# Four instead of three weight pairs by seven products in a SwiGLU unit, their sums written over the loaded words, gate and up completed in PSUM

## The chip, the cores and the metric

The kernel runs on one core of one Trainium2 chip. The metric is the device time of one execution in microseconds. The core has five engines with instruction queues of their own: TensorE (PE, with its weight loads as PEld), VectorE (DVE), ScalarE (ACT), GpSimd (POOL) and SyncE (SP), which here only issues transfers. Each engine executes its queue in the order in which the program was built, and waits at an instruction until the semaphores that it names have come.

## The reference

A hybrid encoder with two layers on 256 tokens of width 2048. Each layer has a mixer (neighbourhood attention with a gated recurrence in layer 0; pooling with grouped attention in layer 1) and then a SwiGLU of hidden width 5632. The change is in the SwiGLU alone:

```
def swiglu(x, w_gate, w_up, w_down):
    return (jax.nn.silu(x @ w_gate) * (x @ w_up)) @ w_down

    x = layer_norm(DN_ALPHA * x + y, ln_mix_g[layer], ln_mix_b[layer])
    f = swiglu(x, ffn_w_gate[layer], ffn_w_up[layer], ffn_w_down[layer])
    x = layer_norm(DN_ALPHA * x + f, ln_ffn_g[layer], ln_ffn_b[layer])
```

## The kernel before

**Numbers in two halves.** Every fp32 operand is split into a high part (a cast to fp32r, on ACT) and a low part (the difference, on DVE), by `split` (L126). A product of two such operands is three matmuls (`mm3`, L287): low by high, high by high, high by low. A matmul is 128 x 128 by 128 x 512. So each weight word that is loaded costs a cast on ACT and a subtraction on DVE before TensorE can use it.

**Chunks and phases.** The hidden width is cut into eleven chunks of 512 columns. `ffn` (L501) takes them in three phases per layer (`PHASES`, L69): three chunks, four, four. After the chunks of a phase come its down projections, which add to the residual. In the first phase a chunk is done by `whole` (L505), gate and up one after the other. In the second and third phase a chunk is a `unit` (L453), which makes gate and up together for both token tiles. There are two layers with two such phases of four units: four stretches, sixteen units.

**A unit.** It has four accumulators, one PSUM bank each: c11 and c21 (gate of the two token tiles), c12 and c22 (up). The contraction over 2048 is cut into eight pairs of 128 rows. A pair is done in one of two ways.

- *By halves*: two loads of 512 KB (`load_half`, L152; tiles raw, whi, wlo), each split by one cast and one subtraction of 128x1024, and eight products, which are 24 matmuls.
- *By seven products* (a scheme of Winograd's kind for a 2 x 2 block product, token tiles and column blocks of x by rows of gate and up): one load of 1 MB (`load_seven`, L431; tile rs), seven weight words instead of four (tiles sh and sl), seven products, which are 21 matmuls. Products p1, p5, p6, p7 go to four side banks; the other three go straight to c11, c12 and c21. The left sides e, f, g, h are made from x once per layer by `forms_of` (L407; tile fm).

`SEVEN` (L72) names the pairs that are done by seven products: 5, 6 and 7. `PAIRS_FIRST`, `PAIRS` and `PAIRS_LAST` (L73 to L75) give the order of the pairs in the first unit of a phase, in the two inner ones, and in the last. L546 sets the pairs by seven products: `SEVEN[:-1]` in the last unit, `SEVEN` in all others.

**load_seven before** (L437 to L447). The words arrive in rs, which has one buffer. ACT casts three words of 512 columns (L442, 128x1536). DVE makes four sums in a tile of its own, z (L443 to L445: 128x1024, 128x512, 128x512), and then the low parts of the first three words (L446). Then the sums are split: a cast of 128x2048 and a subtraction of 128x2048. sh and sl have two buffers each.

**End of a unit** (L481 to L499). ACT copies p1 out of PSUM (L483). DVE then makes ten instructions of 128x512: sums of p1, p5, p6, p7 with the four accumulators into the tiles g0, g1, u0, u1, and two multiplications of silu(gate) by up (L497). ACT takes silu twice (L489, L492). The result of each token tile is transposed by TensorE (`transpose4`, L272, L124) into a side bank and split into yTh and yTl. This is put off by `later`: the first token tile's transposes are called after two halves of the next unit, the second one's after three (L499); a half is counted by `half_done` (L480), and seven products don't count.

**Banks.** The eight banks are two sides of four. The accumulators of a unit are one side, and p1, p5, p6, p7 the other, which is also the side of the two transposed results of the unit before. After a unit the sides change places (L495). The four side banks are asked for at the first pair by seven products (L470).

**What sets the order.** A scheduler orders the instructions of each engine when the program is built, with the priorities of `tc.high_priority` and by a timeline of its own. A buffer is taken again as soon as its last reader is done.

Of the kernel before, what the change touches and what calls it, by code (L numbers as in the profile page):

```python
# [11 lines left out]
F32 = mybir.dt.float32  # L12
# [6 lines left out]
P = 128  # L19
T = 256  # L20
NT = T // P
D = 2048
KT = D // P
NCH = 512
# [56 lines left out]
def trunk(ctx: ExitStack, tc: tile.TileContext, a, out):  # L81
# [44 lines left out]
    def split(hi, lo, src):  # L126
        nc.scalar.copy(hi, src)  # L127
        return nc.vector.tensor_tensor(lo, src, hi.bitcast(F32), op=sub).ins  # L128
# [302 lines left out]
    def load_seven(sp, src, behind):  # L431

        with ExitStack() as order:
            order.enter_context(tc.high_priority(offset=400))
            if behind:
                order.enter_context(tc.issue_after(behind))
            raw = sp.tile([P, 4, NCH], F32, tag="rs", name="rs", bufs=1)  # L437
            hi = sp.tile([P, 7, NCH], F32R, tag="sh", name="sh", bufs=2)
            lo = sp.tile([P, 7, NCH], F32R, tag="sl", name="sl", bufs=2)
            z = sp.tile([P, 4, NCH], F32, tag="z", name="z", bufs=1)  # L440
            last_load[0] = nc.sync.dma_start(raw, src).ins
            nc.scalar.copy(hi[:, :3], raw[:, :3])  # L442
            nc.vector.tensor_tensor(z[:, :2], raw[:, 0:3:2], raw[:, 3:4].to_broadcast([P, 2, NCH]), op=add)  # L443
            nc.vector.tensor_tensor(z[:, 2], z[:, 0], raw[:, 2], op=add)
            nc.vector.tensor_tensor(z[:, 3], z[:, 2], raw[:, 1], op=add)  # L445
            nc.vector.tensor_tensor(lo[:, :3], raw[:, :3], hi[:, :3].bitcast(F32), op=sub)  # L446
            split(hi[:, 3:], lo[:, 3:], z)  # L447
        return lambda i: (hi[:, i, :], lo[:, i, :])


    SEVEN_ORDER = ((0, "11", "p1"), (5, "f", "p6"), (3, "e", "p5"), (4, "g", "p7"), (1, "12", "c11"), (2, "h", "c12"), (6, "22", "c21"))

    def unit(sp, pairs, sevens, w, lhs, forms, yT, opening):  # L453

# [12 lines left out]
        for p in pairs:  # L467
            if p in sevens:
                if "p1" not in b:
                    b.update((n, side_bank(True)) for n in ("p1", "p6", "p5", "p7"))  # L470
                wt = load_seven(sp, w[p], behind.pop(0))
                for i, x, name in SEVEN_ORDER:
                    product(name, forms[p][x], wt(i))
            else:
# [4 lines left out]
                            product(f"c{tok + 1}{n + 1}", lhs(tok, ks[kk]), (hi[:, kk, :], lo[:, kk, :]))  # L479
                    half_done()  # L480
        with tc.high_priority(offset=1000):  # L481
            g0, w_, v, x = (sp.tile([P, NCH], F32, tag=n, name=n, bufs=1) for n in ("g0", "g1", "u0", "u1"))
            nc.scalar.copy(g0, b["p1"])  # L483
            nc.vector.tensor_tensor(w_, g0, b["p6"], op=sub)
            nc.vector.tensor_tensor(v, w_, b["p5"], op=add)
            nc.vector.tensor_tensor(w_, w_, b["p7"], op=add)
            nc.vector.tensor_tensor(x, w_, b["p5"], op=add)
            nc.vector.tensor_tensor(g0, g0, b["c11"], op=add)
            nc.scalar.activation(g0, g0, AF.Silu)  # L489
            nc.vector.tensor_tensor(v, b["c12"], v, op=sub)  # L490
            nc.vector.tensor_tensor(w_, w_, b["c21"], op=add)
            nc.scalar.activation(w_, w_, AF.Silu)  # L492
            nc.vector.tensor_tensor(x, b["c22"], x, op=sub)

            banks["side"] ^= 1  # L495
            for tok, (g, u) in enumerate(((g0, v), (w_, x))):
                nc.vector.tensor_tensor(g, g, u, op=mult)  # L497
                s = slice(tok * P, (tok + 1) * P)
                later.append([2 + tok, lambda g=g, s=s: transpose4(g, yT[0][:, :, s], yT[1][:, :, s], 1000)])  # L499
# [651 lines left out]
```

## Time and profile before

| | us |
|---|---|
| median of 3 runs (2194.17 to 2198.57) | 2197.3 |
| the profiled execution | 2194.88 |
| its span, first to last instruction | 2193.1 |
| loads of raw from in_gu, 512 KB each | 264 loads, 4.7 from issue to landing |
| loads of rs from in_gu, 1 MB each | 44 loads, 5.7 from issue to landing |

The profile is one execution with every instruction's start and duration, the engine, the line of the code and the tiles that it writes and reads. A group's mean is the duration of one instruction; neighbouring instructions of an engine can overlap, so that their starts lie closer together than their durations. A duration can't be added up where this is so: the distance of starts is then the price of one more. The 44 loads of rs are the pairs by seven products: eleven in each of the four stretches. In the span TensorE reads sh from 736 to 871 us, 994 to 1131 us, 1688 to 1823 us and 1946 to 2081 us: these are the four stretches, each some 20 us after its first matmul.

### The profile page before, as it was taken

The numbers are of one execution on the slowest core, as the hardware profiler recorded it, in microseconds if no ns is written. First come the engines' busy times: TensorE is split into PE (matmuls) and PEld (weight loads), VectorE is DVE, ScalarE is ACT, GpSimd is POOL, SyncE is SP. The second block draws the span as 40 slices with busy tenths as digits, with TensorE's granted clock in tenths as the row PEclk, the third lists the DMA queues.
The fourth block names the chain that finished last, engine by engine and source line by source line (L and its number), as shares of the span: only waits on it lengthen the run. The fifth ranks groups of instructions, "written<-read, shape, count | busy, mean of one in ns | idle before, by whom it ended". The sixth has DMA issues, their size and how long they took to land.

```text
span 2193.1 us, 26619 instructions
## 1 busy us (share of the span) xinstructions
PE 2172.0 (99%) x10048; PEld 1804.2 (82%) x10048; DVE 1558.9 (71%) x1952; ACT 1050.4 (48%) x1276; POOL 55.4 (3%) x51
## 2 busy tenths in 40 slices
PE   8999999999999999999999999999999999999997
PEld 7888888888888888888888888888888888888886
DVE  6885688577537787577776776667367896768865
ACT  6445534545435455444445554455335454445441
POOL 0000001000000000000000200000000000000000
PEclk9999999999999999999999999999999999999999
DMA  8555546684736565565548553646456555655573
GB/s 290 162 163 182 167 132 192 197 284 141 234 121 220 187 205 191 189 232 184 194 151 299 171 189 115 223 161 244 150 175 234 181 189 191 220 183 191 176 258 106
DMA packets 112562, 420.64 MB, mean 192 GB/s; under 512 B 13744, under 2 KB 16304, under 8 KB 105520
## 3 DMA queue, kind: packets, MB, share of 16 engines
q1 hardware_dynamic: 112432, 418.93, 57.2%
q8 instruction: 79, 1.29, 0.2%
q14 instruction: 51, 0.42, 0.1%
HBM read 416.78 MB, written 2.10 MB: 191 GB/s over the span
## 4 chain that ended last, share of the span: by engine, by line
PE 93%; DVE 3%; DMA 2%; ACT 1%; issue 1%; SPq 0%; ACTq 0%; DVEq 0%
PE acc L290 45%; PE bside L290 22%; PE aside L290 20%; PE mx L720 1%; DMA raw<-in_gu 1%; DVE wlo L128 1%; PE tr L124 1%; PE mx L290 1%; DMA rs<-in_gu 1%; ACT whi L127 1%; PE mx L766 0%; PE aside L124 0%; PE bside L124 0%; PE mx L976 0%; DVE sl L128 0%
## 5 line engine op out<-in xcount | busy, mean ns | idle before, releaser
L128 DVE TENSOR_TENSOR wlo<-raw,whi 128x1024 fp32r<-128x1024 f32 (+1 forms) x673 | 817.7, 1224 | 439.2 <-ACT whi L127 432.6
L127 ACT CAST whi<-raw 128x1024 fp32r<-128x1024 f32 (+1 forms) x673 | 703.7, 1051 | 818.6 <-PE acc L290 321.9
L290 PE MATMUL acc<-whi,xTl 128*128 128x512 f32 x1056 | 416.7, 395 | 6.7 <-DVE xTl L128 5.5
L290 PE MATMUL acc<-whi,xTh 128*128 128x512 f32 x1056 | 414.6, 393 | 0.0
L290 PE MATMUL acc<-wlo,xTh 128*128 128x512 f32 x1056 | 412.6, 393 | 0.3 <-DVE wlo L128 0.3
L290 PEld LDWEIGHTS acc<-whi,xTl 128*128 128x128 f32 x1056 | 198.9, 188 | 46.9 <-ACT whi L127 6.9
L290 PEld LDWEIGHTS acc<-wlo,xTh 128*128 128x128 f32 x1056 | 199.0, 188 | 41.1 <-DVE wlo L128 0.7
L290 PEld LDWEIGHTS acc<-whi,xTh 128*128 128x128 f32 x1056 | 199.1, 189 | 38.7
L290 PE MATMUL acc<-whi,yTl 128*128 128x512 f32 x512 | 200.7, 392 | 0.1
L290 PE MATMUL acc<-whi,yTh 128*128 128x512 f32 x512 | 199.7, 390 | 0.0
L290 PE MATMUL acc<-wlo,yTh 128*128 128x512 f32 x512 | 197.8, 390 | 0.0
L290 PE MATMUL bside<-whi,xTl 128*128 128x512 f32 x336 | 131.4, 391 | 0.9 <-ACT g L483 0.7
L290 PE MATMUL aside<-whi,xTl 128*128 128x512 f32 x336 | 131.3, 391 | 0.1
L290 PE MATMUL bside<-whi,xTh 128*128 128x512 f32 x336 | 131.0, 390 | 0.0
L290 PE MATMUL aside<-whi,xTh 128*128 128x512 f32 x336 | 131.0, 390 | 0.0
L290 PE MATMUL aside<-wlo,xTh 128*128 128x512 f32 x336 | 128.1, 390 | 0.0
L290 PE MATMUL bside<-wlo,xTh 128*128 128x512 f32 x336 | 128.1, 390 | 0.0
L290 PEld LDWEIGHTS acc<-wlo,yTh 128*128 128x128 f32 x512 | 96.1, 188 | 20.5 <-DVE wlo L128 0.5
L290 PEld LDWEIGHTS acc<-whi,yTl 128*128 128x128 f32 x512 | 96.1, 188 | 19.8 <-DVE yTl L982 0.3
L290 PEld LDWEIGHTS acc<-whi,yTh 128*128 128x128 f32 x512 | 96.2, 188 | 19.3
L128 DVE TENSOR_TENSOR sl<-z,sh 128x2048 fp32r<-128x2048 f32 x44 | 100.7, 2288 | 6.2 <-ACT sh L127 5.6
L442 ACT CAST sh<-rs 128x1536 fp32r<-128x1536 f32 x44 | 65.2, 1483 | 73.3 <-DMA rs<-in_gu 34.6
(260 smaller groups left out, 3117.4 us busy)
## 6 DMA issues: line engine op xcount, KB each, us to landing
raw<-in_gu SPq DMA_DIRECT2D x264, 512.0 KB, 4.7
raw<-in_down SPq DMA_DIRECT2D x176, 512.0 KB, 3.7
raw<-in_ab_in SPq DMA_DIRECT2D x127, 512.0 KB, 4.1
rs<-in_gu SPq DMA_DIRECT2D x44, 1024.0 KB, 5.7
raw<-in_cd_in SPq DMA_DIRECT2D x40, 512.0 KB, 4.3
raw<-in_ab_out SPq DMA_DIRECT2D x32, 512.0 KB, 4.4
raw<-in_cd_out SPq DMA_DIRECT2D x32, 512.0 KB, 4.4
x<-in_xT SPq DMA_DIRECT2D x8, 256.0 KB, 5.9
```

The source lines that it names most:

```text
L124: return nc.tensor.transpose(o, src, eye)
L127: nc.scalar.copy(hi, src)
L128: return nc.vector.tensor_tensor(lo, src, hi.bitcast(F32), op=sub).ins
L290: ins = nc.tensor.matmul(o, lhs[a], rhs[b], start=start and n == 0, stop=stop and n == 2)
L442: nc.scalar.copy(hi[:, :3], raw[:, :3])
L720: nc.tensor.matmul(m[:, 2 * h + s, :], kk[:, h, s * P : (s + 1) * P], qq[:, h, r * P : (r + 1) * P], start=True, stop=True,)
```

## The change

Three things are changed.

1. `SEVEN` becomes (4, 5, 6, 7), and the inner units take their pairs in the order 0, 4, 1, 5, 2, 6, 3, 7. Two new names, `SEVEN_FIRST` and `SEVEN_LAST`, are not used anywhere. The line that chooses the pairs of a unit is as it was, so that the first and the inner units have four pairs by seven products and the last has three: 15 in each stretch, 60 in all, in place of 44. The forms e, f, g, h are made for four pairs.
2. In `load_seven` the tile z is gone. The first three words are split first, and then the four sums are written over the loaded words in rs, which now has two buffers (xs and fs of `forms_of` use them too).
3. At the end of a unit u0 and u1 are gone: c11, c12, c21 and c22 get the sums in PSUM, silu reads PSUM, and the last multiplications read up from PSUM. The side banks are asked for in the order p1, p6, p7, p5.

```
-SEVEN = (5, 6, 7)
+SEVEN = (4, 5, 6, 7)
+SEVEN_FIRST = (5, 6, 7)
+SEVEN_LAST = (5, 6)
 PAIRS_FIRST = (0, 1, 2, 3, 5, 4, 6, 7)
-PAIRS = (0, 1, 5, 2, 3, 6, 4, 7)
+PAIRS = (0, 4, 1, 5, 2, 6, 3, 7)
 PAIRS_LAST = (0, 1, 5, 2, 6, 3, 4, 7)
...
-        xs = sp.tile([P, NT, 2 * n, P], F32, tag="rs", name="xs", bufs=1)
-        fs = sp.tile([P, 4, n, P], F32, tag="z", name="fs", bufs=1)
+        xs = sp.tile([P, NT, 2 * n, P], F32, tag="rs", name="xs", bufs=2)
+        fs = sp.tile([P, 4, n, P], F32, tag="rs", name="fs", bufs=2)
...
-            raw = sp.tile([P, 4, NCH], F32, tag="rs", name="rs", bufs=1)
+            raw = sp.tile([P, 4, NCH], F32, tag="rs", name="rs", bufs=2)
...
-            z = sp.tile([P, 4, NCH], F32, tag="z", name="z", bufs=1)
             last_load[0] = nc.sync.dma_start(raw, src).ins
-            nc.scalar.copy(hi[:, :3], raw[:, :3])
-            nc.vector.tensor_tensor(z[:, :2], raw[:, 0:3:2], raw[:, 3:4].to_broadcast([P, 2, NCH]), op=add)
-            nc.vector.tensor_tensor(z[:, 2], z[:, 0], raw[:, 2], op=add)
-            nc.vector.tensor_tensor(z[:, 3], z[:, 2], raw[:, 1], op=add)
-            nc.vector.tensor_tensor(lo[:, :3], raw[:, :3], hi[:, :3].bitcast(F32), op=sub)
-            split(hi[:, 3:], lo[:, 3:], z)
+            split(hi[:, :3], lo[:, :3], raw[:, :3])
+
+            nc.vector.tensor_tensor(raw[:, 0:4:3], raw[:, 0:3:2], raw[:, 3:4].to_broadcast([P, 2, NCH]), op=add)
+            nc.vector.tensor_tensor(raw[:, 2], raw[:, 0], raw[:, 2], op=add)
+            nc.vector.tensor_tensor(raw[:, 1], raw[:, 2], raw[:, 1], op=add)
+            split(hi[:, 3:], lo[:, 3:], raw)
...
-                    b.update((n, side_bank(True)) for n in ("p1", "p6", "p5", "p7"))
-                wt = load_seven(sp, w[p], behind.pop(0))
+                    b.update((n, side_bank(True)) for n in ("p1", "p6", "p7", "p5"))
+                wt = load_seven(sp, w[p], behind.pop(0) if behind else None)
...
-            g0, w_, v, x = (sp.tile([P, NCH], F32, tag=n, name=n, bufs=1) for n in ("g0", "g1", "u0", "u1"))
-            nc.scalar.copy(g0, b["p1"])
-            nc.vector.tensor_tensor(w_, g0, b["p6"], op=sub)
-            nc.vector.tensor_tensor(v, w_, b["p5"], op=add)
+            g, w_ = (sp.tile([P, NCH], F32, tag=n, name=n, bufs=1) for n in ("g0", "g1"))
+            nc.scalar.copy(g, b["p1"])
+            nc.vector.tensor_tensor(w_, g, b["p6"], op=sub)
+            nc.vector.tensor_tensor(b["c11"], g, b["c11"], op=add)
+            nc.vector.tensor_tensor(g, w_, b["p5"], op=add)
+            nc.vector.tensor_tensor(b["c12"], b["c12"], g, op=sub)
             nc.vector.tensor_tensor(w_, w_, b["p7"], op=add)
-            nc.vector.tensor_tensor(x, w_, b["p5"], op=add)
-            nc.vector.tensor_tensor(g0, g0, b["c11"], op=add)
-            nc.scalar.activation(g0, g0, AF.Silu)
-            nc.vector.tensor_tensor(v, b["c12"], v, op=sub)
-            nc.vector.tensor_tensor(w_, w_, b["c21"], op=add)
-            nc.scalar.activation(w_, w_, AF.Silu)
-            nc.vector.tensor_tensor(x, b["c22"], x, op=sub)
+            nc.vector.tensor_tensor(g, w_, b["p5"], op=add)
+            nc.vector.tensor_tensor(b["c22"], b["c22"], g, op=sub)
+            nc.scalar.activation(g, b["c11"], AF.Silu)
+            nc.vector.tensor_tensor(b["c21"], w_, b["c21"], op=add)
+            nc.scalar.activation(w_, b["c21"], AF.Silu)
...
-            for tok, (g, u) in enumerate(((g0, v), (w_, x))):
+            for tok, (g, u) in enumerate(((g, b["c12"]), (w_, b["c22"]))):
```

The built programs have 9856 matmuls before and 9808 after, 1521 and 1569 two-operand instructions on DVE, and 795 and 779 transfers; ACT has the same number of instructions. Lines move down by up to two: the split's subtraction is L128 before and L130 after, the matmuls L290 and L292, the transposes L124 and L126, the load of rs L441 and L442, the copy of p1 L483 and L485.

The order moves at three places. The first is DVE's queue in the first stretch, where the first unit ends, before the change. sl<-rs are the low parts of the first three words, z the sums, sl<-z their low parts, g and u the end of the unit.

```order
L443 TENSOR_TENSOR z<-rs 128x1024 [waits DMAHW5_49,DVE_49]
L444 TENSOR_TENSOR z<-z,rs 128x512 [waits DVE_49]
L445 TENSOR_TENSOR z<-z,rs 128x512 [waits DVE_49]
L446 TENSOR_TENSOR sl<-rs,sh 128x1536 [waits PE_49,Activation_49]
L484 TENSOR_TENSOR g_6259<-g_6258,aside 128x512 [waits PE_49,Activation_49]
L128 TENSOR_TENSOR sl<-z,sh 128x2048 [waits Activation_49]
```

After the change, DVE's queue at the end of the second unit of the same stretch; `x2` is the same instruction for two pairs in a row.

```order
L130 TENSOR_TENSOR sl<-rs,sh 128x1536 [waits DMAHW1_49,PE_49,Activation_49]
L130 TENSOR_TENSOR sl<-rs,sh 128x1536 [waits DMAHW4_49,PE_49,Activation_49]
L445 TENSOR_TENSOR rs<-rs 128x2x512 [waits DVE_49] x2
L446 TENSOR_TENSOR rs<-rs 128x512 [waits DVE_49] x2
L130 TENSOR_TENSOR wlo<-raw,whi 128x1024 [waits DMAHW3_49,PE_49,Activation_49]
L447 TENSOR_TENSOR rs<-rs 128x512 [waits DVE_49] x2
L487 TENSOR_TENSOR aside<-g_6562,aside 128x512 [waits PE_49,Activation_49]
L130 TENSOR_TENSOR yTl<-bside,yTh 128x4x128 [waits Activation_49]
L130 TENSOR_TENSOR sl<-rs,sh 128x2048 [waits Activation_49] x2
```

Before, the three sums stood ahead of the first subtraction and waited for the load alone. Now they stand behind it, and so behind the cast on ACT and the release of sh by TensorE; two pairs go through these steps side by side.

The second place is TensorE's queue where the results of the second token tile are transposed. Before the change this is early in the second unit, ahead of its first product of p1 (bside<-sh,xTl).

```order
L290 MATMUL aside<-wlo,xTh_3815 128x512
L124 MATMUL bside<-ident,g_6259 128x128 [waits DVE_49]
L124 MATMUL bside<-ident,g_6259 128x128 x3
L290 MATMUL bside<-sh,xTl_3816 128x512
L290 MATMUL bside<-sh,xTh_3814 128x512
```

After the change the transposes of the first unit's result stand at the end of the second unit, behind the last product of p1, whose bank they take; the third unit's first accumulator takes the same bank (bside<-whi).

```order
L292 MATMUL bside<-sl,xTh_3814 128x512 [waits DVE_49]
L292 MATMUL aside<-sl,xTh_3814 128x512
L292 MATMUL aside<-sl,fmh 128x512
L126 MATMUL bside<-ident,g_6252 128x128 [waits Activation_49]
L126 MATMUL bside<-ident,g_6252 128x128 x3
L292 MATMUL bside<-whi,xTl_3816 128x512 [waits DVE_49]
L292 MATMUL bside<-whi,xTh_3814 128x512
L292 MATMUL bside<-wlo,xTh_3814 128x512
L292 MATMUL bside<-whi,xTl_3816 128x512
L292 MATMUL bside<-whi,xTh_3814 128x512
L292 MATMUL bside<-wlo,xTh_3814 128x512
L292 MATMUL bside<-sh,fml 128x512 [waits Activation_49]
```

With pair 4 in second place, the side banks are asked for after two halves, ahead of the call of the second transposes; these therefore wait for the copy of p1 (Activation), and the matmul behind them for the split of what they wrote (DVE). It is so twice in each stretch, in the two inner units.

The third place is ACT's queue there, after the change: the casts of the first three words wait for TensorE and for the load, and the casts of the sums for DVE.

```order
L129 CAST sh<-rs 128x1536 [waits DMAHW1_49,PE_49]
L129 CAST sh<-rs 128x1536 [waits DMAHW4_49,DVE_49,PE_49]
L129 CAST whi<-raw 128x1024 [waits DMAHW3_49,DVE_49,PE_49]
L485 COPY g_6562<-bside 128x512 [waits PE_49]
L129 CAST yTh<-bside 128x4x128 [waits PE_49]
L129 CAST sh<-rs 128x2048 [waits DVE_49] x2
L129 CAST sh<-rs 128x1536 [waits DMAHW1_49,DVE_49,PE_49]
```

The casts of both pairs' sums have moved behind the copy of p1 and the cast of the transposed result. The load of a pair waits, on SP, until the subtraction of 128x2048 of the pair two before it is done, which is the last reader of its buffer of rs; before, it waited for the sums or the subtraction of 128x1536.

More of the change, by code (lines that the diff above doesn't have):

```diff
@@ L436, in load_seven @@
                 order.enter_context(tc.issue_after(behind))
-            raw = sp.tile([P, 4, NCH], F32, tag="rs", name="rs", bufs=1)
+            raw = sp.tile([P, 4, NCH], F32, tag="rs", name="rs", bufs=2)
             hi = sp.tile([P, 7, NCH], F32R, tag="sh", name="sh", bufs=2)
             lo = sp.tile([P, 7, NCH], F32R, tag="sl", name="sl", bufs=2)
-            z = sp.tile([P, 4, NCH], F32, tag="z", name="z", bufs=1)
             last_load[0] = nc.sync.dma_start(raw, src).ins
-            nc.scalar.copy(hi[:, :3], raw[:, :3])
-            nc.vector.tensor_tensor(z[:, :2], raw[:, 0:3:2], raw[:, 3:4].to_broadcast([P, 2, NCH]), op=add)
-            nc.vector.tensor_tensor(z[:, 2], z[:, 0], raw[:, 2], op=add)
-            nc.vector.tensor_tensor(z[:, 3], z[:, 2], raw[:, 1], op=add)
-            nc.vector.tensor_tensor(lo[:, :3], raw[:, :3], hi[:, :3].bitcast(F32), op=sub)
-            split(hi[:, 3:], lo[:, 3:], z)
+            split(hi[:, :3], lo[:, :3], raw[:, :3])
[3 more added lines that the diff above has]
+            split(hi[:, 3:], lo[:, 3:], raw)
         return lambda i: (hi[:, i, :], lo[:, i, :])
-    SEVEN_ORDER = ((0, "11", "p1"), (5, "f", "p6"), (3, "e", "p5"), (4, "g", "p7"), (1, "12", "c11"), (2, "h", "c12"), (6, "22", "c21"))
+    SEVEN_ORDER = ((0, "11", "p1"), (5, "f", "p6"), (3, "e", "p5"), (6, "g", "p7"), (1, "12", "c11"), (2, "h", "c12"), (4, "22", "c21"))
     def unit(sp, pairs, sevens, w, lhs, forms, yT, opening):
```

## The prediction

> **What bounds the kernel now.** First the page: its first rows say which engine is full.
>
> ```profile
> span 2193.1 us, 26619 instructions
> PE 2172.0 (99%) x10048; PEld 1804.2 (82%) x10048; DVE 1558.9 (71%) x1952; ACT 1050.4 (48%) x1276; POOL 55.4 (3%) x51
> ```
>
> TensorE is busy throughout; VectorE has 71% on average. An average over stages doesn't price a change in one of them, so the second view is the windows, cut from one copy of p1 on ScalarE to the next: these are two units of the first stretch.
>
> ```profile
> 752.21 0.58 ACT L483 COPY g<-aside 128x512 f32<-128x512 f32 x1
> ...
> 796.16 0.57 ACT L483 COPY g<-bside 128x512 f32<-128x512 f32 x1
> ...
> 839.37 0.57 ACT L483 COPY g<-aside 128x512 f32<-128x512 f32 x1
> ```
>
> ```profile
> core 0: us, PE busy (x) PEld busy (x) DVE busy (x) ACT busy (x) POOL busy (x), PEclk, DMA share, GB/s
> 752.00:796.00 44.00, 44.00 (x199) 36.42 (x198) 35.41 (x34) 22.86 (x22) 0.00 (x0) 1.00 0.51 169
> 796.00:839.00 43.00, 42.92 (x193) 35.21 (x192) 38.56 (x40) 22.59 (x22) 0.00 (x0) 1.00 0.61 208
> ```
>
> Here VectorE has (35.41 + 38.56) / 87 = 85%, ScalarE 52%. TensorE is the bound, but VectorE is close behind, and the change shifts work from the one to the other. The chain of waits from 740 to 800 us gives TensorE's price:
>
> ```profile
> 755.77 11.56 PE aside L290 x51
> 767.33 0.44 PE bside L124 x4
> ```
>
> 51 matmuls in 11.56 us are **0.2267 us each** (the 0.39 that a group's mean shows is a duration that overlaps its neighbours). Four transposes take 0.44.
>
> VectorE's and ScalarE's prices come from the distance of starts in the timeline of VectorE and from two views by tile:
>
> ```profile
> 754.63 2.29 DVE L128 TENSOR_TENSOR sl<-z,sh 128x2048 fp32r<-128x2048 f32 x1
> 756.84 0.68 DVE L485 TENSOR_TENSOR u<-g,aside 128x512 f32<-128x512 f32 x1
> ...
> 759.23 1.21 DVE L443 TENSOR_TENSOR z<-rs 128x1024 f32<-128x1024 f32 x1
> 760.36 0.68 DVE L487 TENSOR_TENSOR u<-g,aside 128x512 f32<-128x512 f32 x1
> 760.96 0.68 DVE L497 TENSOR_TENSOR g<-g,u 128x512 f32<-128x512 f32 x1
> 761.56 1.75 DVE L446 TENSOR_TENSOR sl<-rs,sh 128x1536 fp32r<-128x1536 f32 x1
> 763.23 0.68 DVE L444 TENSOR_TENSOR z<-z,rs 128x512 f32<-128x512 f32 x1
> ...
> 768.51 1.21 DVE L128 TENSOR_TENSOR wlo<-raw,whi 128x1024 fp32r<-128x1024 f32 x1
> 769.64 0.68 DVE L128 TENSOR_TENSOR yTl<-bside,yTh 128x512 fp32r<-128x512 f32 x1
> ```
>
> ```profile
> L442 ACT CAST sh<-rs x44: 1475/1483/1488, 687.4 to 2055.9; 128x1536 fp32r<-128x1536 f32 x44
> L127 ACT CAST sh<-z x44: 1903/1913/1921, 696.4 to 2066.8; 128x2048 fp32r<-128x2048 f32 x44
> ```
>
> ```profile
> DMA to landing us min/median/max: 4.6/5.7/8.0
> ```
>
> So VectorE needs 0.60 us for 512 columns, 1.13 for 1024, 1.67 for 1536 and 2.21 for 2048; ScalarE 1.48 and 1.91 for a pair's two casts; and a load of rs 5.7 until it lands.
>
> VectorE starts the next instruction 0.08 us before the recorded end of the last. [...] With whole durations one more pair by seven products would cost 4.2 us of VectorE; the distance of starts decides here.
>
> **The change part by part.**
>
> *Fewer matmuls.* The built order has 60 pairs by seven products, not 44: the first and last units take one more too, though the change's name speaks of inner ones. 16 x 3 = 48 matmuls go: 48 x 0.2267 = **10.9 us less**, all on the bounding engine. Sixteen transfers go as well; the queue has room.
>
> *VectorE.* A pair by seven products takes 1.67 + 1.13 + 0.60 + 0.60 + 2.21 = 6.21 us, by halves 2 x 1.13 = 2.26. One more costs 3.95, four in a stretch 15.8, while TensorE's work there falls by 2.7. Per inner unit: before 10 x 1.13 + 3 x 6.21 + 12 x 0.60 (ten at the unit's end, two yTl) = 37.1 us of VectorE; after, 8 x 1.13 + 4 x 6.21 + 7.2 = 41.1, against 180 x 0.2267 + 0.9 = 41.7 of TensorE. The cover that hid VectorE's waits is gone.
>
> *ScalarE* gets 1.48 + 1.91 - 2 x 1.05 = 1.3 us per pair more; with half its time idle it hides that, unless a wait hangs on a single cast (below).
>
> ```profile
> L127 ACT CAST whi<-raw 128x1024 fp32r<-128x1024 f32 x44 | 45.8, 1052 | 48.9 <-PE bside L290 21.9 <-PE aside L290 18.2 <-issue 8.4
> ```
>
> *Forms for four pairs.* Some 2 us of VectorE per layer, beside down projections: nothing.
>
> *Sums in PSUM.* Four instructions per unit now write PSUM, which no row shows. Reading it costs nothing (yTl from a bank and the tiles-only L497 above both take 0.68). Lower end: 0.60 as before. Upper end: the next larger shape, 1.13, on 64 instructions, 34 us. I take 0.60, by the nearest row. Silu from PSUM took 0.59, from a tile 0.63: nothing.
>
> ```profile
> L512 ACT ACTIVATE sil<-acc x12: 590/594/598, 526.0 to 1579.0; 128x512 f32<-128x512 f32 x12
> ```
>
> ```profile
> L489 ACT ACTIVATE g<-g 128x512 f32<-128x512 f32 x3 | 1.9, 632 | 6.0 <-DVE g L488 6.0
> ```
>
> *The order of a pair's preparation.* This is the term that decides. Before, a sum needed the load alone, and rs came free early:
>
> ```profile
> 754.12 0.33 SPq L441 DMA_DIRECT2D rs<-in_gu  x1
> ...
> 768.01 0.33 SPq L441 DMA_DIRECT2D rs<-in_gu  x1
> ```
>
> Issued at 754.12, the pair's first sum ran at 759.23, its last just before the next issue at 768.01. After the change the chain is in series: TensorE releases sh, cast, subtraction, three sums, cast, subtraction: 1.5 + 1.7 + 2.3 + 1.9 + 2.2 = 9.6 us plus handovers, two pairs in step, and only the last subtraction frees rs for the next load. I followed the built order of the first stretch by hand with these prices (0.1 us per handover, 0.4 for a matmul's result), from the first unit's second seven product pair to the last unit's second. TensorE then stands still as follows.
>
> 1. End of the first unit, 3.9 us. Both last pairs go in step. From the release of the first buffer, its low words come at 3.6, the second pair's at 7.8, the second halves at 13.2 and 17.9; TensorE's 66 matmuls are 15.0 us and end at 18.9.
> 2. Late loads, 6.3. The last subtraction is followed by 5.7 of transfer and 1.4 of cast, 7.2 with handovers, and the matmuls in between cover most of it: left are 1.6, 1.3, 2.1 and 1.4.
> 3. VectorE behind those loads, 8.0. What arrives late must pass it together with the end of a unit: five waits of 0.4 to 3.2.
> 4. The second transposes, 6.5. Worked out for the first: with the cast of one pair at 0, the two casts end at 1.4 and 2.8; subtractions at 3.2 and 4.9; sums and a half's 1.13 fill VectorE to 10.7, c11's add to 11.3, yTl to 11.9. TensorE has 6 + 15 + 9 matmuls, ends at 8.6, waits for the copy of p1 (0.57, the rows above) until 9.3, transposes, and waits for yTl until 12.0: 2.8 in all. In the other inner unit it is 3.7.
> 5. Casts that wait for the release of sh with no matmul left to cover them, 1.8.
>
> The sum is 26.5 us per stretch. All four have the same order of queues, so 106. **106 - 10.9 = 95 us more.** The profiled execution took 2194.9 (span 2193.1 and 1.8 around it): 2290. The median of the runs shown is 2.4 above it; I keep 2290.
>
> **The rivals.**
>
> *VectorE by its share alone.* The waits overlap better than the hand count has it, and only VectorE's throughput counts. At today's 85% four more pairs stretch a stretch by 15.8 / 0.85 = 18.6, less 1 us that TensorE is above this pace today: 17.6 x 4 = 70, so 2265. For it: VectorE kept 80 and 90% in the two windows above, with chains much like these. Against it: those chains didn't have the sums behind the cast.
>
> *Everything stays hidden: faster.* If TensorE's lead (seven halves and two pairs made ahead) covers the waits, the 10.9 remains: 2184. It decides at 2.7 us of waiting per stretch: below that it is faster. For it, the rows of 740 to 800 show hardly a wait today. Against it, the second transposes stand on TensorE's own queue, where a lead in weights helps nothing, and they alone cost 6.5.
>
> *The clock.* At the start, after TensorE stood still, its matmuls came 0.43 us apart, half speed; after the longest wait inside the kernel, 1.25 us, they came 0.24 apart once more:
>
> ```profile
> 5.00:12.00 7.00, 5.80 (x14) 4.20 (x15) 4.56 (x7) 4.30 (x7) 0.00 (x0) 1.00 0.99 369
> ```
>
> ```profile
> 8.83 0.63 PE L290 MATMUL acc<-whi,xTl 128*128 128x512 f32 x1
> 9.26 0.63 PE L290 MATMUL acc<-whi,xTh 128*128 128x512 f32 x1
> ```
>
> ```profile
> 1381.15 0.38 PE L290 MATMUL mx<-ptl,dvh 128*128 128x256 f32 x1 [1.25 <-DVE ptl L128]
> ...
> 1385.04 0.40 PE L290 MATMUL acc<-whi,yTh 128*128 128x512 f32 x1
> 1385.28 0.40 PE L290 MATMUL acc<-wlo,yTh 128*128 128x512 f32 x1
> ```
>
> The 14 matmuls of that window lose some 13 x 0.2 = 2.6 us. If each of my waits of 3 us or more (two per stretch) brings it, 8 x 2.6 = 21: 2311; with six per stretch, 62: 2352. I put the case at 2325. [...] No run here shows where the limit lies.
>
> **How the numbers follow.** The hand count 0.60, the share 0.24, the clock 0.06, hidden 0.06, and 0.04 for waits that happen to balance the gain (2.2 to 3.8 us per stretch). A measurement of this kernel tells 0.2%, about 4.4 us, from no change. So slower 0.90, same 0.04, faster 0.06. The prediction is 2290. With loads at 4.6 or 8.0 instead of 5.7, four times per stretch, the hand count gives 2272 to 2327; PSUM writes at their upper end would add up to 34 if all stood on the path. The range takes in the share's case with as much below it: 2230 to 2330.
>
> **What would show it.** 9808 matmuls at the same 0.227 us, and TensorE's busy time some 10 us less beside a longer span. Right: waits of TensorE of about 100 us in total, for sl, sh and yTl, where today's list of its waits has 9, most of it in these three rows; the matmul behind the second transposes waits 1.5 to 3 us, eight times; ScalarE's first cast waits for the load of rs; VectorE in the inner units at 80 to 85% although TensorE waits for it. Wrong: units still 43 to 44 us from one copy of p1 to the next (I expect 49 to 52); VectorE above 95% there (then it is throughput, not order); subtractions or sums into PSUM clearly above 0.68 us; matmuls 0.43 us apart behind waits.
>
> ```profile
> PE acc L290 <- DVE xTl L128: 5.5, 1, 5.5
> PE mx L290 <- DVE ptl L128: 1.2, 1, 1.2
> PE bside L290 <- ACT g L483: 0.7, 1, 0.7
> ```

## The result, with the profile after

| | median, us | lowest to highest | runs |
|---|---|---|---|
| before, beside it | 2196.3 | 2194.17 to 2198.57 | 4 |
| after | 2288.0 | 2286.62 to 2291.47 | 4 |

The ratio is 1.042, with a 95% interval of 1.0407 to 1.0432: slower by 92 us, where the prediction had 2290 and a range of 2230 to 2330. The first two rows of the page after the change:

```profile
span 2286.0 us, 26459 instructions
...
PE 2193.8 (96%) x10000; PEld 1798.9 (79%) x10000; DVE 1622.9 (71%) x2000; ACT 1071.3 (47%) x1276; POOL 55.9 (2%) x51
```

48 matmuls are gone, and TensorE is no longer busy throughout: 99% has become 96%. VectorE has 64 us more work and the same share as before, 71%. What TensorE waits for is read from the list of its waits (us in total, times, longest):

```profile
PE aside L292 <- ACT sh L129: 14.6, 13, 2.7
PE bside L292 <- ACT sh L129: 10.8, 10, 2.2
PE aside L292 <- DVE yTl L130: 8.7, 4, 2.6
PE bside L292 <- DVE yTl L130: 8.2, 4, 2.1
PE bside L292 <- DVE g L490: 7.3, 4, 2.8
PE aside L292 <- DVE g L490: 7.3, 5, 2.9
PE acc L292 <- DVE xTl L130: 5.5, 1, 5.5
PE aside L292 <- DVE sl L130: 4.2, 11, 1.1
```

The row of 5.5 (xTl) is the start of the program and was there before. All others are new: the words of the seven products (sh, sl), the second transposed result (yTl), and banks that VectorE has not yet read out (g L490). The same cut as before, from one copy of p1 on ScalarE to the next, shows the stretch of the prediction's windows. First the copies in the timeline of ScalarE, then the windows:

```profile
751.39 0.58 ACT L485 COPY g<-aside 128x512 f32<-128x512 f32 x1 [2.39 <-PE aside L292]
798.58 0.59 ACT L485 COPY g<-bside 128x512 f32<-128x512 f32 x1 [0.76 <-PE bside L292]
850.51 0.59 ACT L485 COPY g<-aside 128x512 f32<-128x512 f32 x1 [0.76 <-PE aside L292]
```

```profile
core 0: us, PE busy (x) PEld busy (x) DVE busy (x) ACT busy (x) POOL busy (x), PEclk, DMA share, GB/s
751.40:798.60 47.20, 42.94 (x179) 32.21 (x178) 40.19 (x39) 22.65 (x20) 0.00 (x0) 1.00 0.43 156
798.60:850.50 51.90, 43.71 (x189) 34.15 (x188) 40.98 (x40) 24.07 (x21) 0.00 (x0) 1.00 0.46 157
```

The two inner units take 47.2 and 51.9 us instead of 44.0 and 43.2, with VectorE busy for (40.19 + 40.98) / 99.1 = 82% of them: less than the 85% that it had before, when TensorE did not wait. How one of the long waits comes about is read from the chain of waits between 852 and 872 us (start, us, what the chain goes through):

```profile
852.55 1.91 ACT sh L129
...
854.48 2.31 DVE sl L130
...
856.80 4.67 DMA rs<-in_gu
...
861.57 1.49 ACT sh L129
...
864.76 0.68 DVE g L486
...
866.49 1.22 DVE rs L445
867.71 0.60 DVE g L488
...
869.89 0.69 DVE rs L446
870.58 0.61 DVE bside L489
871.19 0.60 DVE g L490
...
871.83 15.04 PE aside L292 x58
```

Cast, subtraction, load into the buffer that the subtraction has freed, cast, and then VectorE, where the sums over the loaded words and the sums that end the unit stand in one row: TensorE has waited 2.87 us when it goes on at 871.83. Nothing in this chain is long by itself, but its pieces follow one another, and the matmuls that TensorE had in the meantime ended 2.87 us too early.

**Where the 92 us are.** The starts of TensorE's instructions, taken one by one in both traces, give the whole difference of the spans, 92.9 us. The wait of 5.5 at the start, which both have, is left out:

| | us |
|---|---|
| TensorE idle before an instruction: 75.3 in 90 waits, was 4.3 in 15 | 71.0 |
| the matmul before a wait, recorded with 0.39 us where matmuls otherwise start 0.227 apart | 12.4 |
| half clock (last section) | 9.0 |
| matmuls with no wait of their own; 7.2 of it on those just after a waiting one, from whose start the next is some 0.34 away instead of 0.227 | 9.7 |
| transposes | 0.9 |
| fewer matmuls | -10.1 |
| sum | 92.9 |

### The profile page after: what moved, and what is told of

Read it like the earlier page. It is cut to its first block, busy times and chain, and to the rows that moved or that the text cites. A ratio compares the mean times of both kernels' runs of the same rounds, so it can differ in the third digit from the quotient of the medians.

```text
span 2286.0 us, 26459 instructions
## 1 busy us (share of the span) xinstructions
PE 2193.8 (96%) x10000; PEld 1798.9 (79%) x10000; DVE 1622.9 (71%) x2000; ACT 1071.3 (47%) x1276; POOL 55.9 (2%) x51
## 4 chain that ended last, share of the span: by engine, by line
PE 84%; DVE 8%; DMA 4%; ACT 3%; issue 2%; SPq 0%; ACTq 0%; DVEq 0%
PE acc L292 45%; PE bside L292 18%; PE aside L292 16%; DVE sl L130 3%; DMA rs<-in_gu 2%; ACT sh L129 2%; PE mx L722 1%; PE tr L126 1%; DMA raw<-in_gu 1%; DVE wlo L130 1%; PE mx L292 1%; DVE rs L445 1%; ACT whi L129 0%; DVE rs L446 0%; DVE rs L447 0%
## 5 line engine op out<-in xcount | busy, mean ns | idle before, releaser
L130 DVE TENSOR_TENSOR wlo<-raw,whi 128x1024 fp32r<-128x1024 f32 (+1 forms) x641 | 779.0, 1225 | 461.8 <-ACT whi L129 452.3
L129 ACT CAST whi<-raw 128x1024 fp32r<-128x1024 f32 (+1 forms) x641 | 671.3, 1051 | 815.9 <-PE acc L292 313.2
L292 PE MATMUL acc<-whi,xTl 128*128 128x512 f32 x1056 | 417.6, 396 | 8.1 <-DVE xTl L130 5.5
L292 PE MATMUL acc<-whi,xTh 128*128 128x512 f32 x1056 | 415.4, 393 | 0.0
L292 PE MATMUL acc<-wlo,xTh 128*128 128x512 f32 x1056 | 413.3, 393 | 0.0
L130 DVE TENSOR_TENSOR sl<-rs,sh 128x1536 fp32r<-128x1536 f32 (+1 forms) x120 | 241.4, 2023 | 74.4 <-ACT sh L129 73.8
L129 ACT CAST sh<-rs 128x1536 fp32r<-128x1536 f32 (+1 forms) x120 | 201.3, 1694 | 166.7 <-DMA rs<-in_gu 66.7
L292 PEld LDWEIGHTS acc<-whi,xTl 128*128 128x128 f32 x1056 | 199.4, 189 | 48.6 <-ACT whi L129 7.0
L292 PEld LDWEIGHTS acc<-wlo,xTh 128*128 128x128 f32 x1056 | 199.2, 189 | 40.1
L292 PEld LDWEIGHTS acc<-whi,xTh 128*128 128x128 f32 x1056 | 199.5, 189 | 38.5
L292 PE MATMUL acc<-whi,yTl 128*128 128x512 f32 x512 | 201.2, 393 | 1.9 <-DVE g L491 1.7
L292 PE MATMUL acc<-whi,yTh 128*128 128x512 f32 x512 | 199.9, 390 | 0.0
L292 PE MATMUL acc<-wlo,yTh 128*128 128x512 f32 x512 | 198.0, 390 | 0.0
L292 PE MATMUL aside<-whi,xTl 128*128 128x512 f32 x272 | 108.6, 399 | 16.8 <-DVE yTl L130 8.7
L292 PE MATMUL bside<-whi,xTl 128*128 128x512 f32 x272 | 108.6, 399 | 15.6 <-DVE yTl L130 8.2
L292 PEld LDWEIGHTS acc<-whi,yTl 128*128 128x128 f32 x512 | 96.2, 188 | 22.3 <-DVE g L491 2.6
L292 PEld LDWEIGHTS acc<-wlo,yTh 128*128 128x128 f32 x512 | 96.2, 188 | 20.4 <-DVE wlo L130 0.5
L292 PEld LDWEIGHTS acc<-whi,yTh 128*128 128x128 f32 x512 | 96.3, 188 | 19.1
L292 PE MATMUL bside<-wlo,xTh 128*128 128x512 f32 x272 | 106.1, 395 | 1.4 <-DVE wlo L130 1.4
L292 PE MATMUL bside<-whi,xTh 128*128 128x512 f32 x272 | 107.3, 395 | 0.0
L292 PE MATMUL aside<-whi,xTh 128*128 128x512 f32 x272 | 107.1, 394 | 0.0
L292 PE MATMUL aside<-wlo,xTh 128*128 128x512 f32 x272 | 105.6, 394 | 0.0
```

The lines of the kernel that those rows point to most:

```text
L292: ins = nc.tensor.matmul(o, lhs[a], rhs[b], start=start and n == 0, stop=stop and n == 2)
```

## The experiments

Twelve kernels ran, each against the kernel before on the same chip. In all rows the ratio is to the kernel before:

| | median, us | ratio, 95% interval |
|---|---|---|
| after | 2288.0 | 1.0407 to 1.0432 |
| e1, second transposes early | 2261.3 | 1.0281 to 1.0311 |
| e2, sums apart, one rs | 2271.6 | 1.0323 to 1.0358 |
| e3, 44 sets | 2216.4 | 1.0076 to 1.0106 |
| e4, e1 and e2 | 2252.8 | 1.0242 to 1.0273 |
| e5, before and 62 us of VectorE | 2215.2 | 1.0072 to 1.0103 |
| e6, e4 with two rs | 2231.7 | 1.0147 to 1.0177 |
| e7, after with three rs | 2268.6 | 1.0316 to 1.0350 |
| e8, 52 sets | 2274.2 | 1.0339 to 1.0370 |
| e9, e5 with another tile size | 2210.8 | 1.0049 to 1.0079 |
| e10, before and the new end alone | 2197.0 | 0.9989 to 1.0008 |
| e11, e7 and e1 | 2265.6 | 1.0295 to 1.0326 |
| e12, before and the new preparation alone | 2215.6 | 1.0070 to 1.0103 |

A set is one pair by seven products. e6, e7 and e11 leave out the low part of the forms: their matmuls read the high part twice, TensorE has as many matmuls as in the changed kernel, and VectorE one subtraction of 2.29 us less per layer. The two theories: the order in which a set is prepared makes TensorE wait (the prediction), or VectorE has too much work (the rival of its share).

### e1: both second transposes after two halves

```
-                later.append([2 + tok, lambda g=g, s=s: transpose4(g, yT[0][:, :, s], yT[1][:, :, s], 1000)])
+                later.append([2, lambda g=g, s=s: transpose4(g, yT[0][:, :, s], yT[1][:, :, s], 1000)])
```

> The changed kernel, with the second token tile's transposes called after two halves of the next unit, as the first one's are (60 pairs by seven products, sums in place). The theory of the order: the eight waits for yTl and the copies of p1 go, 17 + 2 us of waits and some 2.5 us of refilling behind them, and perhaps two or three of the six stretches of half clock at 1.5 us each; 2288 becomes about 2265 (2255 to 2275). The theory of VectorE's throughput: VectorE's work is the same and its pace sets the end, so no change, 2284 to 2292.

2261.3, 26.7 us less than after: as the order theory has it. The waits for yTl are gone from the list of TensorE's waits, which now begins:

```profile
PE aside L292 <- ACT sh L129: 17.4, 18, 2.0
PE bside L292 <- ACT sh L129: 13.5, 12, 2.3
```

VectorE's work is the same as in after, so this part of the loss is not its throughput. But the waits for sh have grown from 25.4 to 30.9: some of what is taken away comes back at the next place.

### e2 and e4: the sums in a tile of their own again

e2 is the changed kernel with the old preparation of a set; e4 has the edit of e1 as well.

```
-            raw = sp.tile([P, 4, NCH], F32, tag="rs", name="rs", bufs=2)
+            raw = sp.tile([P, 4, NCH], F32, tag="rs", name="rs", bufs=1)
+            z = sp.tile([P, 4, NCH], F32, tag="z", name="z", bufs=1)
...
-            split(hi[:, :3], lo[:, :3], raw[:, :3])
+            nc.scalar.copy(hi[:, :3], raw[:, :3])
+            nc.vector.tensor_tensor(z[:, :2], raw[:, 0:3:2], raw[:, 3:4].to_broadcast([P, 2, NCH]), op=add)
...
+            nc.vector.tensor_tensor(lo[:, :3], raw[:, :3], hi[:, :3].bitcast(F32), op=sub)
+            split(hi[:, 3:], lo[:, 3:], z)
```

> The changed kernel with the sums in a tile of their own again (rs and z with one buffer each, the sums ahead of the first subtraction), 60 pairs, late second transposes, sums in PSUM at the unit's end. The theory of the order: the waits for sh, for the unit's end behind late loads and part of those for sl go, 14 to 18 us of 26 per stretch; 2288 becomes about 2225 (2205 to 2245). The theory of throughput: the same work for VectorE, 2284 to 2292.

> The changed kernel with both: second transposes after two halves, and the sums in a tile of their own; 60 pairs. The theory of the order: nearly all waits go, what is left is VectorE at 41 of 42 us per inner unit; 2190 to 2220. The theory of throughput: VectorE keeps its 80 to 85%, 2260 to 2290.

2271.6 and 2252.8: 16 and 35 us less than after, neither theory's number. The list of ScalarE's waits shows why, first for e2, then for e4 (the cast of the first three words is L444 here):

```profile
ACT sh L444 <- DMA rs<-in_gu: 132.8, 44, 8.2
```

```profile
ACT sh L444 <- DMA rs<-in_gu: 125.7, 45, 5.5
```

With the old preparation there is one buffer for rs, and for 60 sets instead of 44 the load into it comes too late. The edit exchanges one wait for another, so it could not price the sums alone; e6 does.

### e3: the changed kernel with 44 sets

```
-SEVEN = (4, 5, 6, 7)
+SEVEN = (5, 6, 7)
...
-PAIRS = (0, 4, 1, 5, 2, 6, 3, 7)
+PAIRS = (0, 1, 5, 2, 3, 6, 4, 7)
```

> The changed kernel with three pairs by seven products and the old order of pairs (44 loads of rs), sums in place, end of the unit in PSUM. The theory of the order: the preparation in series has 14 us per pair in place of 10, so most of it is covered; 2198 to 2225. The theory of throughput: VectorE's work is that of the kernel before, 2194 to 2200. If the writes to PSUM or the sums in place cost by themselves, more than 2225.

2216.4: 20 us slower than before although it has the same matmuls, and 72 less than after. So the preparation or the end of the unit costs something even with the old number of sets, and the 16 further sets, with the order of pairs that makes the second transposes late, cost 72 net, some 82 before the matmuls that they save.

### e10 and e12: the end and the preparation, each alone

e10 is the kernel before with the whole new end of a unit, e12 the kernel before with the new `load_seven` and two buffers for rs; both as in the change's diff.

> The kernel before with the new end of a unit alone (the sums end in PSUM, in the new order; 44 sets, sums of words in their own tile). The prediction costs it at nothing: 2194 to 2200. If the 20 us of e3 come from the end (the banks of a unit are released later, since their sums stand later in VectorE's row): 2207 to 2218.

> The kernel before with the new preparation of a set alone (sums in the load's tile behind the first cast and subtraction, two buffers for rs; 44 sets, old end of a unit). If the 20 us of e3 come from the order of the preparation (the prediction's term): 2207 to 2217. If they come from the end of the unit: 2194 to 2202.

e10 is the same as before (0.9989 to 1.0008): sums that end in PSUM cost nothing here. e12 has 2215.6, the 20 us of e3 within what the intervals allow. In its list of TensorE's waits, the largest rows behind the start are banks that wait for a sum of the unit's end, L485, which in VectorE's row stands behind the second subtractions of two sets (4.49 us in the timeline):

```profile
PE aside L292 <- DVE g L485: 4.6, 4, 1.6
PE bside L292 <- DVE g L485: 3.9, 3, 1.6
```

So the loss at 44 sets belongs to the new order of the preparation.

### e5 and e9: VectorE's work without the order

The kernel before with 104 instructions of 512 columns that nothing waits for. e5 and e9 differ in the size of the tile they write.

```
+    def extra():
+        st = sm.tile([P, 6], F32, tag="junk", name="junk", bufs=1)
+        nc.vector.bn_stats(st, probe[0])
...
             split(hi[:, 3:], lo[:, 3:], z)
+            extra()
+            extra()
...
                 nc.vector.tensor_tensor(g, g, u, op=mult)
+                if tok:
+                    extra()
```

In e9 the tile is `[P, 16]`, of which the first six columns are written.

> The kernel before, with 26 further VectorE instructions per stretch that nothing waits for (statistics of 512 columns of x, taken as 0.60 us each by the rows of the same width): two behind each pair by seven products, one behind each unit's end. That is 15.6 us of VectorE per stretch, what the change adds by the prediction's count, with the order of loads, casts and sums of before. Theory that the order and the waits of the preparation cost the time (the prediction's): little of it shows, 2197 to 2212. Theory that VectorE's throughput costs it (the rival of the share): a stretch is 15 to 18 us longer, 2255 to 2270.

> The kernel of e5 (before, with 104 further VectorE instructions that nothing waits for), but the small tile they write is 64 bytes per partition instead of 24. In e5 TensorE hardly waited; its matmuls came 0.2304 us apart in the first 3000, ahead of the first further instruction, against 0.2276 in the kernel before. Theory that the 24 bytes, which displace every tile behind them, made e5 longer and that the further VectorE work costs nothing: 2192 to 2200. Theory that the further VectorE work cost it: 2211 to 2218.

2215.2 and 2210.8. The first is 3 us above the order theory's range and 40 below that of throughput; the second lies at the lower end of the range given to the further VectorE work, so by its number the size of the tile was not the cause. The trace of e9 shows where the added work went. The view of the tile gives 104 times 0.69 us by duration; VectorE's busy time is 62 us longer than before (104 x 0.60). Its instructions are called in all four units of a stretch, but in the order that was built all 26 of a stretch run before the first unit's copy of p1, and none in the inner units. It is so in all four stretches, and in e5. First the tile alone, in the first unit of the first stretch and in the two inner ones, then all work of that first unit:

```profile
L435 DVE BATCH_NORM_STATS2 junk<-xTh x104: 681/686/697, 686.7 to 1966.9; 128x6 f32<-128x512 f32 x104
```

```profile
core 0: us, DVE busy (x) ACT busy (x), PEclk, DMA share, GB/s
687.00:758.20 71.20, 17.61 (x26) 0.00 (x0) 1.00 0.68 234
758.20:847.50 89.30, 0.00 (x0) 0.00 (x0) 1.00 0.55 185
```

```profile
687.00:758.20 71.20, 71.20 (x314) 58.74 (x313) 68.02 (x73) 35.28 (x30) 0.00 (x0) 1.00 0.68 234
```

VectorE is busy for 68.02 of 71.20 us, 96%, and TensorE throughout. TensorE's list of waits has one row of more than 2 us behind the start's:

```profile
PE aside L290 <- ACT g L491: 2.8, 2, 2.0
```

Both of these waits (at 848 and 1805 us) come some 90 us after the last added instruction of their stretch. The rest of the 13 is a slower rate of the matmuls themselves, which begins at the program's start, long before the first added instruction at 686.7 us: the 3000th matmul is already 5.4 us late. This is taken up in the last section.

So 85% is no pace that VectorE can't exceed, which is what the rival of its share took: it was busy for 96% of 71 us without a wait of TensorE. What the two runs don't show is how much room it has in the inner units, whose sets cost most (e8), since no added work ran there. There other rows speak against throughput as the whole cause: the kernel before had VectorE at 90% in its second inner unit (38.56 of 43.00 us in the prediction's windows) with TensorE busy, the changed one has it at 79 to 85% in all eight inner units and TensorE waits. And at the same sets and the same work of VectorE, or nearly so in e6, e1 takes 27 us off the changed kernel and e6 56.

### e6: sums apart, early transposes, two buffers for rs

The edit is shown against e4.

```
-            raw = sp.tile([P, 4, NCH], F32, tag="rs", name="rs", bufs=1)
+            raw = sp.tile([P, 4, NCH], F32, tag="rs", name="rs", bufs=2)
...
-        hi, lo = split_tile(sp, [P, 4, n, P], fs, "fm")
+        hi = lo = sp.tile([P, 4, n, P], F32R, tag="fmh", name="fmh", bufs=1)
+        nc.scalar.copy(hi, fs)
```

> The kernel of e4 (sums apart from the load's tile, both second transposes after two halves) with a second buffer for rs. The room is made by leaving out the low part of the forms: their matmuls read the high part twice, so 2 of 3 products of a form are the same work on other numbers. Theory that the wait for a load into the single rs costs the time (in e4 ScalarE's first cast waits 125 us for it): 2200 to 2230. Theory that VectorE's throughput or the two buffers of sh and sl do: as e4, 2245 to 2256.

2231.7, just above the range of the single buffer's theory and 21 less than e4: the load into the single buffer was the wait. Against e1, which has the same two buffers and early transposes but the sums over the loaded words (and whole forms), it is 29.5 less: that is the price of the new order at 60 sets, where it was 18 at 44. The first rows of its waits after the start's:

```profile
PE aside L292 <- DVE wlo L130: 4.7, 4, 1.2
PE bside L292 <- DVE wlo L130: 4.7, 4, 1.2
PE bside L292 <- ACT sh L129: 2.9, 8, 1.0
```

It is still 36 us slower than before, which with the 10.1 us of saved matmuls makes 46 of waits and what they bring: TensorE's idle time is 35.2 instead of 4.3 us, in 62 waits instead of 15, again without the start's. The two inner units of the first stretch, in one window:

```profile
755.57:848.35 92.78, 87.05 (x380) 69.19 (x381) 82.59 (x80) 47.69 (x44) 0.00 (x0) 1.00 0.51 179
```

VectorE is busy for 82.59 of 92.78 us, 89% (89 to 92% in all eight inner units). At this share its amount of work may cost part of the 46; no run here separates that from its order.

### e7 and e11: a third buffer for rs with the sums in place

```
-            raw = sp.tile([P, 4, NCH], F32, tag="rs", name="rs", bufs=2)
+            raw = sp.tile([P, 4, NCH], F32, tag="rs", name="rs", bufs=3)
```

Both with the forms of e6; e11 has the edit of e1 as well.

> The changed kernel with a third buffer for rs, the low part of the forms left out as in e6. The prediction's steps 2 and 3 (late loads 6.3, VectorE behind them 8.0 per stretch) should go, 57 us in all, the others stay: 2231, from 2225 to 2260 if part of them turns into waits for the two buffers of sh. Theory that VectorE's throughput costs the time: 2280 to 2292.

> The kernel of e7 (changed kernel, three buffers for rs, low part of the forms left out) with both second transposes after two halves, as e1. If the two edits act on separate waits: 2268.5 less 26 = 2242, from 2237 to 2247. If what each of them takes away is waited for elsewhere (the two buffers of sh and sl, VectorE's row): 2248 to 2262. Throughput of VectorE alone: 2260 or more.

2268.6 and 2265.6. e7 takes back 19.5 of the 57 that the hand count gave to late loads, and e11 takes nothing off e1 (2261.3), which has one buffer less. The first lies between the theories' ranges, the second in that of VectorE's throughput; but e6 has as many sets and as much work for VectorE as e11, and takes 34 us less. What each edit frees is waited for elsewhere. In e11 the list of TensorE's waits begins with the low words of a half, wlo, which in after were late once; bside has a row of the same size:

```profile
PE aside L292 <- DVE wlo L130: 8.3, 4, 2.3
```

The timeline of VectorE before such a wait, which ends at 814.0 us:

```profile
808.09 1.76 DVE L130 TENSOR_TENSOR sl<-rs,sh 128x1536 fp32r<-128x1536 f32 x1 [1.03 <-ACT sh L129]
809.76 0.68 DVE L447 TENSOR_TENSOR rs<-rs 128x512 f32<-128x512 f32 x1
810.36 0.68 DVE L489 TENSOR_TENSOR g<-g,bside 128x512 f32<-128x512 f32 x1
810.96 1.22 DVE L446 TENSOR_TENSOR rs<-rs 128x1024 f32<-128x1024 f32 x1
812.10 0.68 DVE L448 TENSOR_TENSOR rs<-rs 128x512 f32<-128x512 f32 x1
812.70 1.22 DVE L130 TENSOR_TENSOR wlo<-raw,whi 128x1024 fp32r<-128x1024 f32 x1
```

VectorE works without a break and does the words of two sets and the end of a unit before the half that TensorE needs first. Over the unit it has time (41.85 of 51.3 us, 82%); at this place it doesn't.

### e8: the inner units alone with four sets

```
-                    sevens = SEVEN[:-1] if c == chunks[-1] else SEVEN
+                    sevens = SEVEN_LAST if c == chunks[-1] else SEVEN_FIRST if c == chunks[0] else SEVEN
```

> The changed kernel with four pairs by seven products in the inner units alone and three and two in the first and last unit, as the change's name says: 52 sets, 24 fewer matmuls saved (5.4 us). The end of a stretch's first unit (3.9 per stretch by the hand count) is shorter, the last unit has a set less behind the late loads; the inner units keep steps 2 to 4. Order theory: 2255 to 2275. If the loss goes by the number of sets alone (e3 with 44: 2216, the change with 60: 2288), half way: 2252. If it sits in the inner units alone: 2280 or more.

2274.2, at the upper end of the order theory. The eight sets of the first and last units cost 14 us, the eight of the inner units 58 (2274 - 2216): the loss comes mostly with the inner units, where four sets meet the end of the unit before and its transposes. It doesn't all fall there: in the trace of after TensorE is idle for 4 to 5 us in a stretch's first inner unit, 4 to 8 in its second, and 5 to 6 in its last unit. No kernel here was faster than the one before.

## Why the prediction was right

- **Fewer matmuls, 10.9 less**: right, 10.1 by the starts; 60 sets, not 52, were built and ran.
- **VectorE, 41.1 us of work per inner unit**: right (40.2 and 41.0 busy in the windows). Its throughput alone is not what costs the time: e1 and e6.
- **Sums in PSUM at 0.60, range up to 1.13**: right. The sums that write PSUM took 0.69 to 0.70 us by duration where those that write a tile took 0.68 to 0.69, some 1 us over 64 of them, and e10 shows no change of time.
- **The order of the preparation, 106**: the mechanism is right and its places too. The first stretch has the counted waits at the end of the first unit, behind the late loads, for yTl and for sh. Step by step the sizes are less good.
  - *Step 4, the second transposes*, 26 of waiting in all: the waits for yTl are 16.9 and those of the transposes for the copy of p1 1.8. e1 took 26.7 us off, which is more than these waits, though the waits for sh grew by 5.5; that the two numbers agree is luck in part.
  - *Step 1, the end of the first unit*, 3.9 per stretch: 2.5 idle in the first stretch (752 to 763 us).
  - *Steps 2 and 3, late loads and VectorE behind them*, 57 in all: not a part that can be taken away by itself. A third buffer gave 19.5 (e7), or nothing once the transposes were early (e11), and sums apart with two buffers 29.5 (e6 against e1). The steps were worked out as a sum of separate waits; they are one queue.
- **The price of a late load, 5.7 us**: too high. That is the median of before; after the change it is 4.85, the 4.9 of the row below. At this price the prediction's own working, with four late loads per stretch, gives 13.6 us less, 2276.

```profile
rs<-in_gu SPq DMA_DIRECT2D x60, 1024.0 KB, 4.9
```

- **Two errors of the sum cancel.** Waits, with the longer record of the matmul before each, were 71.0 + 12.4 = 83 us, not 106. Two things weren't in the sum: the half clock, 9.0, and slower matmuls, most of them after a wait, 9.7. That 2290 lies 2 us from 2288 is luck; the direction and a loss of this size are not.
- **Waits that balance the gain**: a slip. With 4.4 us on either side of 10.9 they are 1.6 to 3.8 us per stretch, not 2.2 to 3.8; no other number hangs on it.
- **The rival of VectorE's share, 2265**: its premise, a pace of 85%, fell with the 96% in e9, and e6 does the same sets in 2231.7; that its time was only 1% off is luck. A part of the loss may still be VectorE's amount of work (e6).
- **The rival of the clock**: right in part: matmuls 0.43 us apart behind waits, which the prediction names as a sign that it is wrong, came six times. It gave the case 0.06, for waits of 3 us or more; that shorter waits leave the clock alone was not shown. The longest wait after the change was 2.87 us, and about 2 us of idle time were enough (last section).
- **Units of 49 to 52 us**: the second inner unit of each stretch took 49.9 to 51.9, the first only 46.7 to 48.1.

The 92 us in order, each step measured along one path: the late second transposes 27 (after to e1), the sums behind the first subtraction 29.5 (e1 to e6), and 46 that the sixteen further sets cost even then, less 10.1 for the matmuls. Along another path the parts would come out differently, since the same waits answer to several edits (e7 and e11). What the 46 hang on isn't settled: VectorE's amount of work, its order and the two buffers of sh and sl are all left, and no run has a third buffer for these.

## What to carry to other kernels

Price the removal of work on the bounding engine against the order in which the other engines prepare its operands: 10.9 us of TensorE were bought with 16 longer preparations, and what these wait for in the buffers and queues that they share cost 103 (92.9 + 10.1). An engine at 80% on average can still be late at one place (e11: VectorE busy for 82% of a unit, and TensorE waits up to 2.3 us for wlo). Added work that nothing waits for (e5, e9) can tell its throughput from its order, but only where it runs: a scheduler may put it where there is room, so look for it in the trace before reading its price. An edit that writes a result over its own input frees a tile and makes a chain of what ran side by side, so count what the freed tile's reader now waits for.

## What the runs showed of the hardware that was not expected

**Half clock after waits of about 2 us.** In the timeline of TensorE after the change, behind the wait of 2.87 us:

```profile
871.83 0.50 PE L292 MATMUL aside<-whi,xTl 128*128 128x512 f32 x1 [2.87 <-DVE g L490]
...
873.15 0.63 PE L292 MATMUL aside<-wlo,xTh 128*128 128x512 f32 x1
873.58 0.63 PE L292 MATMUL aside<-whi,xTl 128*128 128x512 f32 x1
...
876.74 0.39 PE L292 MATMUL aside<-sl,fmh 128*128 128x512 f32 x1
876.96 0.39 PE L292 MATMUL aside<-whi,xTl 128*128 128x512 f32 x1
```

The matmuls start 0.43 apart from 873.15 on and 0.227 apart again at 876.74; a window cut there shows the granted clock:

```profile
873.02:876.43 3.41, 3.41 (x10) 2.67 (x9) 3.41 (x5) 0.61 (x1) 0.00 (x0) 0.50 0.65 201
```

The trace after the change has six such stretches, each of 3.413 us, each costing about 1.5 us. Their distances are whole multiples of 3.4133 us (873.02 to 1040.27 is 49 of them), so they lie on a fixed grid. Sorted by how long TensorE was idle in the cell of the grid just before, over the nine traces that have such stretches (after, e1, e2, e4, e6, e7, e8, e10, e11): below 1.4 us none began (one in e1 lasted two cells); from 1.4 to 1.6, 1 of 17; to 1.8, 4 of 15; to 2.0, 18 of 22; and from 2.0 on all 32. In the five other traces no cell reaches 1.8 us, and there is no such stretch. So a cell that was idle for 1.8 us, a little over half of it, was enough in most cases. The prediction's case of the clock has it behind single waits of 3 us or more; after the change no wait behind the start's was longer than 2.87 us, and there were six such stretches.

**A wait of TensorE costs about 0.28 us on top of its idle time** in the trace after the change: 0.16 by the recorded end of the matmul before, and 0.12 on the matmul after (9.1 us over 78 waits). Many short waits are dearer than their idle time says.

**Matmuls at another rate in e5 and e9.** In the first 3000 matmuls, those that did not wait started 0.2276 us apart in the kernel before and in all other kernels, 0.2304 in e5 and 0.2293 in e9, at the same granted clock. One piece of the chain of waits that has the same 41 matmuls, first before, then e9:

```profile
407.90 9.32 PE acc L290 x41
```

```profile
410.48 9.45 PE acc L290 x41
```

What both kernels have and no other has is a further small tile in a pool that lies ahead of others, of 24 and 64 bytes per partition. That this displacement is the cause was not shown: with 64 bytes the rate was still slower.
